# The last piece's residual on TensorE, shared pair products, and row tiles for the compressed values, in a two-mixer decoder layer

## The chip, the cores and the metric

One core of a Trainium2 chip runs the whole layer in one launch. The metric is the device time in microseconds (us), the median over runs. TensorE is written PE in the profile (its weight loads PEld), VectorE DVE, ScalarE ACT, GpSimd POOL; SP is the engine whose queue issues nearly all DMAs.

## The reference, cut to what matters

A sequence of 512 tokens, width 1024, passes one layer. One input projection `h = x @ w_in + b_in` feeds two token mixers and their gates; a sum goes through one output projection, a residual and a layer norm:

```python
o_a = nsa_attention(...) * silu(z_a)            # mixer A, 8 heads of 64
o_b = rmsnorm(hgrn2(q_b, f_b, i_b)) * silu(z_b) # mixer B, 4 heads of 128
y = sigmoid(gm_a) * (o_a @ w_branch_a) + sigmoid(gm_b) * (o_b @ w_branch_b)
out = layer_norm(alpha * x + y @ w_out, ln_g, ln_b)
```

Mixer A sums three attentions (compressed blocks, selected blocks, window) with gates per head. The compressed branch has 31 keys and values per group of four heads, made by a small network from blocks of 32 tokens: `pc = masked_softmax(q @ kc.T * scale)`, then `pc @ vc`. Mixer B works in chunks of 64 tokens with the running sum b of the log forget gates in a chunk: `attn = tril(qe @ ke.T)` with `qe = q * exp(b)`, `ke = k * exp(-b)`, `o = attn @ v`, and a state carried from chunk to chunk.

## The kernel before, in words

Sequence positions lie on the free axis as 4 tiles of 128. The large products are made of three TensorE matmuls in the rounded type fp32r, from values split into hi (`A.copy`, a cast on ACT) and lo (`V.tensor_tensor`, the rest, on DVE) by `split2`: hi*hi, hi*lo, lo*hi. Smaller products are plain fp32; the trace shows each of those as two matmul records.

TensorE's instructions and all DMAs keep the order of the program; on ACT and DVE a scheduler places them. The program's backbone is a row of weight tiles: `proj` (line 254) takes tile i, loads tile i+3 into one of three stream buffers, splits tile i+2 and issues 24 matmuls. Inside it `weave.tick()` runs after every 6 matmuls: generators (`hgrn`, `cmp_kv`, `cmp_scores`, `attn_scores`, `attn_values`) put their own instructions there, and the table `D` (line 67) says after how many ticks each goes on. The time of a matmul group in this stream is thus laid out by hand.

`hgrn` (line 364) treats one head of mixer B. Chunks come in pairs of 64 columns. For the products inside pairs, lines 403 to 408 issue six fp32 matmuls: two of 128 columns for the first chunks (weights `ke`), four of 64 columns for the second (weights `e1`). Masked copies on DVE (lines 410 to 415) put the causal part into `attn_sb`.

`cmp_kv` (line 498) makes the compressed keys `kcB` and values. The values are copied by eight small instructions into the block tile `vcB` (128 x 512, zero elsewhere, lines 529 to 536) and split into hi and lo (540). `cmp_probs` makes probabilities and splits them. `attn_values` (line 683) then makes four outputs of 128 x 512, each by three fp32r matmuls of 512 columns (lines 688 to 695), one output per tick.

After the 16 gate tiles (lines 836 to 842) comes the loop over `BRANCH` (line 873): eight tiles of branch weights, each 24 matmuls, order b b b a a b a a. Each output is evacuated on DVE (line 892); those of branch a are added to b (896) and split into y[kt] (898). In the same loop the output weights are loaded (`load_out(n)`, 877), and two tiles later `split_out(n - 2)` (864) takes each row's mean away (ACT with accumulation, 859; 861), casts hi (ACT, 868) and makes lo (DVE, 869). `split_out(6)` and `split_out(7)` come behind the loop. Taking row means from weights and residual makes the rows of the sum have mean zero, so the layer norm has only a scale to find.

The last stage (line 918) has four token tiles tt. Tile 0 runs kt by kt for both halves at once; the others half by half. The last tile is cut into 512, 256 and 256 columns. Behind each piece DVE adds the residual (937), takes statistics (938) and multiplies by the gain (940). At the end: aggregate (942), square root on ACT (945), reciprocal (946), the gain for the last piece (948), two normalizing instructions of 512 columns (950) and a store of 256 KB after each. Working tiles come from a pool `t2` of 67 buffers, PSUM from four pools of two banks: pa, pss, pst, pso.

Of the kernel before, what the change touches and what calls it, by code (L numbers as in the profile page):

```python
# [9 lines left out]
F32 = mybir.dt.float32  # L10
# [12 lines left out]
EPS = 1e-5  # L23

# [22 lines left out]
def _columns(name):  # L47

    c = np.arange(_COLS[name], _COLS[name] + 128)
    if name[0] == "q" and name[1] != "b" or name[:2] == "za":  # L50
# [17 lines left out]
         r0=5, p0=4, p1=11, p2=2, b0=1, a0=1, a1=1, a2=1, a3=1, a4=2, a5=1, s0=17, s2=0, s3=1)  # L68
# [27 lines left out]
def layer_kernel(ctx: ExitStack, tc: tile.TileContext, xT, xn, w0, wi, wf, wv, small, brow, consts,  # L96
# [145 lines left out]
    vcB = cst.tile([P, 4, 128], F32, name="vcB")  # L242
    G.memset(vcB, 0.0)
# [120 lines left out]
    def hgrn(h):  # L364
# [3 lines left out]
        bc, kc, qc = chunks(b), chunks(k), chunks(qs[h])  # L368
# [9 lines left out]
        yield D["h2"]  # L378
        A.activation(e2, e2, AF.Exp)
        A.activation(e1, e1, AF.Exp)  # L380
        A.activation(eb, b, AF.Exp)
        ke = T2(256)
        kev = ke.rearrange("p (t s) -> p t s", s=64)
        A.activation(kev, bc[:, :, 0], AF.Exp, scale=-1.0)
# [5 lines left out]
        qeM, qeo = T2(), T2(256)  # L390
        ebc, qmc = chunks(eb), chunks(qeM)
        qov = qeo.rearrange("p (t s) -> p t s", s=64)
# [17 lines left out]
        for v in range(2):  # L410
            V.copy_predicated(chunks(at[0:64])[:, v:4:2, 0],
                              tri[0:64, 0:64].unsqueeze(1).to_broadcast([64, 2, 64]),
                              chunks(pst_[64 * v:64 * v + 64])[:, v:4:2, 0])
        V.copy_predicated(chunks(at)[:, :, 1], tri[:, 64:128].unsqueeze(1).to_broadcast([P, 4, 64]),
                          chunks(pst_)[:, :, 1])
# [23 lines left out]
        A.activation(sq, po, AF.Square)  # L439
        A.copy(o, po)  # L440
# [55 lines left out]
    mvs, ready, vcp = [None, None], set(), []  # L496

    def cmp_kv():
# [30 lines left out]
        for g in range(2):  # L529
            for m in range(4):  # L530
                r = 32 * (2 * (m % 2) + g)
                dst, src = vcB[r:r + 32, m, 64 * g:64 * g + 64], ps[r:r + 32, 64 + 64 * g:128 + 64 * g]
                if m % 2:
                    V.tensor_copy(dst, src)
                else:
                    A.copy(dst, src)
# [56 lines left out]
    def cmp_scores():  # L593

        while "cmp" not in ready:
            yield 1
        pg = PS(), PS()
        for m in range(4):
            for g in range(2):
                gs = slice(64 * g, 64 * g + 64)  # L600
                T.matmul(pg[g][32 * m:32 * m + 32], kcB[gs], qraw[m][gs], start=True, stop=True)
        sT = T2(), T2()
        A.copy(sT[0], pg[0])
        V.tensor_copy(sT[1], pg[1])
        yield D["p2"]
        ss = T2(), T2()
        s6 = [s.rearrange("p (i m g n) -> p g i m n", i=4, m=2, g=2) for s in ss]
        for g in range(2):
            ps = transpose4(sT[g])
            p4 = ps.rearrange("p (i c m n) -> p c i m n", i=4, c=2, m=2)  # L610
            for c in range(2):
                V.tensor_tensor(s6[c][:, g], p4[:, c], cmask.unsqueeze(2).to_broadcast([P, 4, 2, 32]), ALU.add)
            yield 1
        for c in range(2):
            weave.start(cmp_probs(c, ss[c]), 2 * c)

    def cmp_probs(c, s):
        s3 = s.rearrange("p (x n) -> p x n", n=32)
        mx = SM(16, "mx")
# [8 lines left out]
        for m in range(2):  # L628
            mxm = mx.rearrange("p (i m g) -> p i m g", i=4, m=2)[:, :, m]
            V.tensor_tensor(mxm, mxm, gv.rearrange("p i (g m) b -> p i g m b", g=2)[:, :, :, 2 * c + m, 0], ALU.mult)  # L630
# [3 lines left out]
        PTc[c] = T2(dt=F32R), T2(dt=F32R)  # L634
        split2(ps, *PTc[c])
# [47 lines left out]
    def attn_values():  # L683
# [3 lines left out]
        yield D["b0"]  # L687
        for m in range(4):
            po = PO()
            hi, lo = (t[:, 128 * m:128 * m + 128] for t in vcp)  # L690
            T.matmul(po, hi, PTc[m // 2][0], start=True, stop=False)
            T.matmul(po, hi, PTc[m // 2][1], start=False, stop=False)
            T.matmul(po, lo, PTc[m // 2][0], start=False, stop=True)
            A.copy(asum[:, m], po)
            yield 1
# [139 lines left out]
    gm = {}  # L835
    for i in range(8):
        for c in "ab":
            name = "g%s%d" % (c, i)
            ps, m = proj(name)
            gm[name] = T2()  # L840
            with tc.issue_after(exps[-1]):
                A.activation(gm[name], ps, AF.Tanh, bias=hbias[:, m:m + 1], scale=0.5)


    wo, woraw = [], {}
    lg, lbn = [T2(), T2()], [T2(), T2()]

    def load_out(kt):
        if kt < 8:
# [13 lines left out]

    def split_out(kt):
        hl = [(T2(dt=F32R), T2(dt=F32R)) for _ in range(2)]
        nm = minus_mean(woraw[kt])
# [4 lines left out]

    y, rb = [], {}
    for n, (mix, m0) in enumerate(BRANCH):
# [3 lines left out]
        load_out(n)  # L877
# [22 lines left out]
        if n >= 2:  # L900
            split_out(n - 2)
    split_out(6)
    split_out(7)
# [14 lines left out]
    for tt in range(4):  # L918
        c = slice(128 * tt, 128 * tt + 128)
        last = tt == 3  # L920
        cuts = [(0, 0, 512), (1, 0, 256), (1, 256, 512)] if last else [(0, 0, 512), (1, 0, 512)]
        bst = SM(6 * len(cuts), "bst")
        xr = res[tt]
        bank = (PT, PO, PA, PS)[tt]
        pso_ = [bank() for _ in cuts[:2]] + ([PT()] if last else [])
        seq = [(u, kt) for u in range(len(cuts)) for kt in range(8)]
        if tt == 0:
            seq = [(u, kt) for kt in range(8) for u in range(2)]
        for u, kt in seq:
            hf, a, b = cuts[u]  # L930
            hi, lo = wo[kt][hf]
            ps = pso_[u][:, 0:b - a]
# [3 lines left out]
            if kt == 7:  # L936
                V.scalar_tensor_tensor(xr[hf][:, a:b], ps, 0.5, xr[hf][:, a:b], ALU.mult, ALU.add)
                V.bn_stats(bst[:, 6 * u:6 * u + 6], xr[hf][:, a:b])  # L938
                if not (last and u == 2):
                    V.tensor_tensor(xr[hf][:, a:b], xr[hf][:, a:b], lg[hf][:, a:b], ALU.mult)  # L940
        ag = SM(2, "ag")
        V.bn_aggr(ag, bst[:, 0:6 * len(cuts)])
# [4 lines left out]
        if last:  # L947
            V.tensor_tensor(xr[hf][:, a:b], xr[hf][:, a:b], lg[hf][:, a:b], ALU.mult)
# [84 lines left out]
```

## Time and profile before

| | us |
|---|---|
| median of 3 runs | 438.39 (437.7 to 438.88) |
| the profiled execution | 437.94 |
| its span in the profile | 436.1 |
| around the span | 1.84 |
| PE busy | 428.6 (98% of the span) |
| DVE / ACT / POOL busy | 304.3 / 245.2 / 16.3 |
[...]

The span is from the first to the last instruction on the core. Matmuls are pipelined, so their single durations overlap; the chain of waits gives the time of a group of them in the stream. The time of a line is read from the view that groups instructions by line and shape.

### The profile page before, as it was taken

To read this page: it belongs to the slowest core of one execution; us is meant where nothing else is said; L and a number is where in the kernel's file an instruction comes from. 1 tells how busy PE (TensorE), PEld (TensorE's weight loads), DVE (VectorE), ACT (ScalarE), POOL (GpSimd) and SP (SyncE) were. 2 spreads that over 40 slices of the span, in tenths; PEclk is the share of its full clock that TensorE was granted. 3 is DMA by queue.
4 is the path that set the end of the run, shared out by engine and by line. 5 is a ranking of instruction groups with operands and counts; after the bars stand their busy time and mean duration, and the time that the engine had idled before them with its cause. 6 is when DMAs were issued, how large, how long until landed. Compare 5 with 4: busy or idle time off the path is not lost.

```text
span 436.1 us, 6086 instructions
## 1 busy us (share of the span) xinstructions
PE 428.6 (98%) x2185; PEld 359.6 (82%) x2185; DVE 304.3 (70%) x629; ACT 245.2 (56%) x490; POOL 16.3 (4%) x27
## 2 busy tenths in 40 slices
PE   9999999999999999999999999999999999999994
PEld 8888888888898878888888888888888888877884
DVE  5915669986887577976665666578755768875395
ACT  4434624613447553768866666688864646569300
POOL 2000000000010220000000010001001100000000
PEclk9999999999999999999999999999999999999998
DMA  8995400352330554132112211111212462153022
GB/s 270 396 357 173 176 0 1 86 145 74 114 95 0 170 155 157 51 116 78 48 48 59 87 51 48 50 48 48 99 48 98 167 220 87 57 157 134 1 102 92
DMA packets 20879, 47.57 MB, mean 109 GB/s; under 512 B 2929, under 2 KB 4593, under 8 KB 20849
## 3 DMA queue, kind: packets, MB, share of 16 engines
q1 hardware_dynamic: 20560, 46.92, 32.1%
q8 instruction: 17, 0.28, 0.3%
q10 hardware_dynamic: 288, 0.26, 0.2%
q14 instruction: 14, 0.11, 0.1%
HBM read 41.93 MB, written 2.10 MB: 101 GB/s over the span
## 4 chain that ended last, share of the span: by engine, by line
PE 93%; DVE 5%; ACT 1%; issue 0%; DVEq 0%; ACTq 0%
PE pa L104 59%; PE pss L104 15%; PE pso L104 12%; PE pst L108 5%; PE pst L104 2%; DVE t L869 1%; DVE t L892 1%; DVE t L148 1%; ACT t L147 1%; DVE t L896 1%; DVE wlo L148 0%; DVE t L950 0%; DVEq L1029 0%; DVE sm_nm L861 0%; DVE sm_bst L938 0%
## 5 line engine op out<-in xcount | busy, mean ns | idle before, releaser
L104 PE MATMUL pa<-t,whi 128*128 128x512 f32 x640 | 201.6, 396 | 0.0
L104 PEld LDWEIGHTS pa<-t,whi 128*128 128x128 f32 x640 | 117.0, 188 | 24.5 <-issue 1.2
L104 PE MATMUL pa<-t,wlo 128*128 128x512 f32 x320 | 125.1, 391 | 0.0
L104 PEld LDWEIGHTS pa<-t,wlo 128*128 128x128 f32 x320 | 60.1, 188 | 13.1
L147 ACT CAST whi<-wraw 128x1024 fp32r<-128x1024 f32 x46 | 48.2, 1047 | 33.7 <-PE pa L104 20.1
L148 DVE TENSOR_TENSOR wlo<-wraw,whi 128x1024 fp32r<-128x1024 f32 x46 | 57.8, 1261 | 12.0 <-ACT whi L147 11.8
L664 DVE CUSTOM_DVE_ANT_0 t<-pss,t 128x512 f32<-128x512 f32 (+3 forms) x64 | 30.1, 488 | 24.0 <-PE pss L104 24.0
L148 DVE TENSOR_TENSOR t<-pst,t 128x512 fp32r<-128x512 f32 x42 | 28.9, 690 | 17.3 <-ACT t L147 17.2
L667 ACT ACTIVATE t<-t,sm_mn 128x512 f32<-128x512 f32 (+3 forms) x64 | 35.8, 560 | 9.1 <-DVE sm_mn L664 7.4
L104 PE MATMUL pso<-t,t 128*128 128x512 f32 (+2 forms) x170 | 36.9, 352 | 0.0
L104 PE MATMUL pa<-t,t 128*128 128x512 f32 (+1 forms) x168 | 36.7, 375 | 0.0
L104 PE MATMUL pss<-t,t 128*128 128x512 f32 (+4 forms) x238 | 36.1, 307 | 0.0
L147 ACT CAST t<-pst 128x512 fp32r<-128x512 f32 x42 | 24.3, 579 | 20.4 <-PE pst L108 20.3
L104 PEld LDWEIGHTS pa<-t,t 128*128 128x128 f32 x168 | 30.3, 188 | 5.6
L104 PEld LDWEIGHTS pss<-t,t 128*128 128x128 f32 (+1 forms) x238 | 29.3, 176 | 3.7 <-DMA wraw<-in_wf_dram 0.4
L104 PEld LDWEIGHTS pso<-t,t 128*128 128x128 f32 x170 | 28.2, 196 | 4.2
L108 PE MATMUL pst<-con,t 128*128 128x128 f32 x189 | 28.6, 272 | 0.0
L108 PEld LDWEIGHTS pst<-con,t 128*128 128x128 f32 x189 | 23.2, 141 | 4.2 <-DVE t L148 0.2
L148 DVE TENSOR_TENSOR t<-t,t 128x512 fp32r<-128x512 f32 (+1 forms) x22 | 14.2, 666 | 13.5 <-ACT t L147 13.4
L104 PE MATMUL pso<-t,vv 128*128 128x512 f32 x80 | 23.1, 410 | 0.0
L147 ACT CAST t<-t 128x512 fp32r<-128x512 f32 (+1 forms) x22 | 12.7, 603 | 12.9 <-DVE t L896 12.7
L104 PE MATMUL pss<-t,whi 128*128 128x512 f32 x64 | 19.7, 389 | 0.0
(164 smaller groups left out, 532.5 us busy)
## 6 DMA issues: line engine op xcount, KB each, us to landing
wraw<-in_wf_dram SPq DMA_DIRECT2D x38, 512.0 KB, 3.6
wraw<-in_wbr_dram SPq DMA_DIRECT2D x8, 512.0 KB, 3.5
t<-in_wout_dram SPq DMA_DIRECT2D x16, 256.0 KB, 3.8
t<-in_w_dram SPq DMA_DIRECT2D x15, 256.0 KB, 5.5
t<-t SPq DMA_DIRECT2D x48, 64.0 KB, 2.0
t<-in_wi_dram SPq DMA_DIRECT2D x8, 256.0 KB, 6.1
t<-in_xn_dram SPq DMA_DIRECT2D x8, 256.0 KB, 7.1
out_dram<-t SPq DMA_DIRECT2D x8, 256.0 KB, 2.1
```

The costliest lines, as they stand in the source:

```text
L104: return tc.keep_in_program_order(nc.tensor.matmul(*a, **k))
L108: return tc.keep_in_program_order(nc.tensor.transpose(*a, **k))
L147: A.copy(dst_hi, src)
L148: V.tensor_tensor(dst_lo, src, dst_hi.bitcast(F32), ALU.subtract)
L664: V.tensor_tensor_reduce(out=p[:, c], in0=ps[:, c], in1=amask[:, 512 - n:512], op0=ALU.add, op1=ALU.min, scale=-0.125, scalar=3.0e38, accu ...
L667: A.activation(p[:, c], p[:, c], AF.Exp, bias=mn[:, k], scale=-1.0, accum_out=den[:, k])
L869: V.scalar_tensor_tensor(lo, raw, nm, hi.bitcast(F32), ALU.add, ALU.subtract)
L892: V.scalar_tensor_tensor(r, gm["g%s%d" % (mix, m)], 1.0, ps, ALU.add, ALU.mult)
L896: V.tensor_tensor(r, r, rb[m], ALU.add)
```

## The change

1. Mixer B: the first chunk's query is scaled by exp(-(b_end - b)) and by 2^-64 (`FIRST`), so that both chunks of a pair use the same weights `e1`: four fp32 matmuls of 128 columns and one masked copy of 128 x 512. The output of first chunks is scaled back when it leaves PSUM.
2. Compressed values: one copy to a 128 x 128 `vcB`; probabilities stay fp32, in rows 32m + n per group; eight fp32 matmuls with 32 rows, 64 weight columns and 512 moving columns, into four banks (two of pso, two of pst), and four copies behind them.
3. Output weights: load, row mean and split of each kt are issued three tiles earlier; the first begin in the gate loop, the last split stands at BRANCH tile 6.
4. The last piece: twice the residual is split into hi and lo and added by TensorE with an identity (two more matmuls of 256 columns); ACT sums the squares from PSUM; DVE applies the gain from PSUM. Squares of the other two pieces are also summed on ACT instead of DVE statistics. Four normalizing instructions of 256 columns and four stores of 128 KB.
5. `D["s0"]`, the delay of `attn_scores`, is 18 ticks for 17.

```diff
+AHEAD = 1
+FIRST = 2.0 ** -64
...
-        ke = T2(256)
-        A.activation(kev, bc[:, :, 0], AF.Exp, scale=-1.0)
+        A.activation(qpc[:, :, 0], chunks(e1)[:, :, 0], AF.Exp, scale=-1.0)
...
-        V.tensor_tensor(qov, qc[:, :, 1], ebc[:, :, 1], ALU.mult)
-        V.tensor_tensor(kev, kev, kc[:, :, 0], ALU.mult)
-        V.tensor_tensor(qmc[:, :, 0], qc[:, :, 0], ebc[:, :, 0], ALU.mult)
-        V.tensor_tensor(qmc[:, :, 1], qov, ebc[:, :, 0, 63:64].to_broadcast([P, 4, 64]), ALU.mult)
+        V.tensor_tensor(qpc[:, :, 1], qc[:, :, 1], ebc[:, :, 1], ALU.mult)
+        V.scalar_tensor_tensor(qpc[:, :, 0], qc[:, :, 0], FIRST, qpc[:, :, 0], ALU.mult, ALU.mult)
+        V.scalar_tensor_tensor(qmc[:, :, 0], qc[:, :, 0], FIRST, ebc[:, :, 0], ALU.mult, ALU.mult)
+        V.tensor_tensor(qmc[:, :, 1], qpc[:, :, 1], ebc[:, :, 0, 63:64].to_broadcast([P, 4, 64]), ALU.mult)
...
-        for u in range(2):
-            T.matmul(chunks(pst_)[:, 2 * u:2 * u + 2, 0], ke[:, 128 * u:128 * u + 128],
-                     qmc[:, 2 * u:2 * u + 2, 0], start=True, stop=True)
         for t in range(4):
-            T.matmul(pst_[:, 128 * t + 64:128 * t + 128], e1[:, 128 * t:128 * t + 128],
-                     qeo[:, 64 * t:64 * t + 64], start=True, stop=True)
+            c = slice(128 * t, 128 * t + 128)
+            T.matmul(pst_[:, c], e1[:, c], qp[:, c], start=True, stop=True)
...
-        A.activation(sq, po, AF.Square)
-        A.copy(o, po)
+        A.activation(chunks(o)[:, :, 0], chunks(po)[:, :, 0], AF.Identity, scale=1.0 / FIRST)
+        A.copy(chunks(o)[:, :, 1], chunks(po)[:, :, 1])
+        A.activation(sq, o, AF.Square)
...
-        for g in range(2):
-            for m in range(4):
-                r = 32 * (2 * (m % 2) + g)
...
+        A.copy(vcB, ps[:, 64:192])
         ready.add("cmp")
-        yield 2
-        vcp.extend((T2(dt=F32R), T2(dt=F32R)))
-        split2(vcB.rearrange("p m d -> p (m d)"), *vcp)
...
-        PTc[c] = T2(dt=F32R), T2(dt=F32R)
-        split2(ps, *PTc[c])
+        PTc[g] = T2()
+        A.copy(PTc[g], ps)
...
+        pc = [PO(), PO(), PT(), PT()]
+        for g in range(2):
+            for m in range(4):
+                rows = slice(32 * m, 32 * m + 32)
+                T.matmul(pc[m][64 * g:64 * g + 64], vcB[rows, 64 * g:64 * g + 64], PTc[g][rows],
+                         start=True, stop=True)
         for m in range(4):
-            po = PO()
-            hi, lo = (t[:, 128 * m:128 * m + 128] for t in vcp)
-            T.matmul(po, hi, PTc[m // 2][0], start=True, stop=False)
-            T.matmul(po, hi, PTc[m // 2][1], start=False, stop=False)
-            T.matmul(po, lo, PTc[m // 2][0], start=False, stop=True)
-            A.copy(asum[:, m], po)
-            yield 1
+            A.copy(asum[:, m], pc[m])
+        yield 1
...
+    def out_ahead(n):
+        n += AHEAD
+        load_out(n + 2)
+        if 0 <= n < 8:
+            split_out(n)
+        if 0 <= n + 1 < 8:
+            mean_out(n + 1)
...
+            out_ahead(2 * i + "ab".index(c) - 16)
...
-        load_out(n)
...
-        if n >= 2:
-            split_out(n - 2)
-    split_out(6)
-    split_out(7)
+        out_ahead(n)
...
+    V.tensor_copy(eye, ident)
+    A.activation(r2h, rlast, AF.Identity, scale=2.0)
+    V.scalar_tensor_tensor(r2l, rlast, 2.0, r2h.bitcast(F32), ALU.mult, ALU.subtract)
...
+        V.scalar_tensor_tensor(xr[hf][:, a:b], ps, 0.5, xr[hf][:, a:b], ALU.mult, ALU.add)
+        A.activation(junk[:, 0:b - a], xr[hf][:, a:b], AF.Square, accum_out=ss[:, u:u + 1])
+        V.tensor_tensor(xr[hf][:, a:b], xr[hf][:, a:b], lg[hf][:, a:b], ALU.mult)
+    V.tensor_scalar(ss[:, 0:1], ss[:, 0:1], 1.0 / DM, EPS, ALU.mult, ALU.add)
+    V.scalar_tensor_tensor(ss[:, 1:2], ss[:, 1:2], 1.0 / DM, ss[:, 0:1], ALU.mult, ALU.add)
+    ps = PT()[:, 0:256]
+    run = outputs(ps, 3, 1, 256, 512)
+    next(run)
+    T.matmul(ps, eye, r2h, start=False, stop=False)
+    T.matmul(ps, eye, r2l, start=False, stop=False)
+    for _ in run:
+        pass
+    with tc.issue_after(nat):
+        A.activation(junk[:, 0:256], ps, AF.Square, scale=0.5, accum_out=ss[:, 2:3])
+        A.activation(ss[:, 3:4], ss[:, 2:3], AF.Sqrt, scale=1.0 / DM, bias=ss[:, 1:2])
+    V.scalar_tensor_tensor(rlast, ps, 0.5, lg[1][:, 256:512], ALU.mult, ALU.mult)
+    V.reciprocal(ss[:, 3:4], ss[:, 3:4])
+    for hf, a, b in ((0, 0, 256), (0, 256, 512), (1, 0, 256), (1, 256, 512)):
+        V.scalar_tensor_tensor(xr[hf][:, a:b], xr[hf][:, a:b], ss[:, 3:4], lbn[hf][:, a:b], ALU.mult, ALU.add)
+        dma(out[384:512, 512 * hf + a:512 * hf + b], xr[hf][:, a:b])
```

`outputs` issues the same three matmuls per kt as before for one piece; `mean_out` is the first half of the old `split_out`.

## Rows read from the trace of the kernel before

**Rows 1.** The page: busy time of each engine, share of the span, instructions.

```profile
PE 428.6 (98%) x2185; PEld 359.6 (82%) x2185; DVE 304.3 (70%) x629; ACT 245.2 (56%) x490; POOL 16.3 (4%) x27
```

**Rows 2.** The page: the chain that ended last, by engine.

```profile
PE 93%; DVE 5%; ACT 1%; issue 0%; DVEq 0%; ACTq 0%
```

**Rows 3.** Chain of waits, 68 to 140 us: start, length, what, records.

```profile
76.52 1.29 PE pss L104 x12
...
90.47 0.67 PE pss L104 x6
...
136.82 0.99 PE pss L104 x8
```

**Rows 4.** Chain of waits, whole span, around the compressed branch.

```profile
161.18 1.38 PE pss L104 x16
...
199.15 0.68 PE pso L104 x3
```

**Rows 5.** Stretches: busy (instructions) of PE, PEld, DVE, ACT, POOL; then clock, DMA share, GB/s.

```profile
330.00:340.00 10.00, 10.00 (x49) 8.17 (x48) 4.47 (x7) 4.06 (x7) 0.00 (x0) 1.00 0.41 142
350.00:360.00 10.00, 10.00 (x46) 8.28 (x45) 5.74 (x10) 4.31 (x9) 0.00 (x0) 1.00 0.66 213
390.00:400.00 10.00, 9.72 (x42) 7.51 (x41) 6.59 (x12) 9.20 (x18) 0.00 (x0) 1.00 0.60 216
434.00:435.00 1.00, 0.00 (x0) 0.00 (x0) 0.00 (x0) 0.00 (x0) 0.00 (x0) 0.50 0.76 285
```

**Rows 6.** Timeline, 391 to 396 us: start, length, what, [idle before, releaser].

```profile
392.05 4.07 DVE L869 SCALAR_TENSOR_TENSOR t<-t,sm_nm,t 128x512 fp32r<-128x512 f32 x6
392.06 0.19 PEld L104 LDWEIGHTS pst<-t,t 128*128 128x128 f32 x1 [0.33 <-ACT t L868]
392.85 3.32 PEld L104 LDWEIGHTS pst<-t,t 128*128 128x128 f32 x15 [0.60 <-DVE t L869]
```

**Rows 7.** Chain of waits, 380 to 437 us: its end.

```profile
427.12 2.89 PE pst L104 x24
...
430.04 0.44 DVE t L937
...
431.23 0.30 ACT sm_rs L945
...
431.56 0.17 DVE sm_rs L946
```

**Rows 8.** Groups by line and shape: busy, mean ns | idle before.

```profile
L439 ACT ACTIVATE t<-pso 128x512 f32<-128x512 f32 x4 | 2.4, 599 | 7.6 <-PE pso L104 7.6
L937 DVE SCALAR_TENSOR_TENSOR t<-pss,t 128x512 f32<-128x512 f32 x1 | 0.7, 685 | 0.0
L937 DVE SCALAR_TENSOR_TENSOR t<-pst,t 128x256 f32<-128x256 f32 x1 | 0.4, 425 | 1.5 <-PE pst L104 1.5
```

**Rows 9.** Timelines: ACT with accumulation; DVE's last work; SP's last stores; SP's loads.

```profile
299.02 0.50 ACT L667 ACTIVATE t<-t,sm_mn 128x256 f32<-128x256 f32 x1
299.42 0.19 ACT L667 ACTIVATION_READ_ACCUMULATOR t<-t,sm_mn 128x1 f32 x1
...
431.76 1.42 DVE L950 SCALAR_TENSOR_TENSOR t<-t,sm_rs,t 128x512 f32<-128x512 f32 x2
...
432.54 0.99 SPq L111 DMA_DIRECT2D out_dram<-t  x2
...
385.61 0.38 SPq L111 DMA_DIRECT2D t<-in_lng_dram  x1
386.08 0.38 SPq L111 DMA_DIRECT2D t<-in_lnb_dram  x1
```

**Rows 10.** The stores: issue (min/median/max ns) and landing (us); ACT's table loads.

```profile
L111 SPq DMA_DIRECT2D out_dram<-t x8: 332/333/348, 415.5 to 433.2; - x8
...
DMA to landing us min/median/max: 2.0/2.1/3.6
...
L144 ACT ACT_TABLE_LOAD x6 | 7.7, 1283 | 1.7 <-PEq L1021 1.7
```

More of the change, by code (lines that the diff above doesn't have):

```diff
@@ L241, in layer_kernel @@
     asum = cst.tile([P, 4, 512], F32, name="asum")
-    vcB = cst.tile([P, 4, 128], F32, name="vcB")
-    G.memset(vcB, 0.0)
+    vcB = cst.tile([P, 128], F32, name="vcB")
     split(0)
@@ L494, in cmp_hidden @@
         mvs[a] = mv
-    mvs, ready, vcp = [None, None], set(), []
+    mvs, ready = [None, None], set()
     def cmp_kv():
@@ L832, in layer_kernel @@
         zs[name] = z
[L835 to L842, printed above, removed]
     wo, woraw = [], {}
-    lg, lbn = [T2(), T2()], [T2(), T2()]
     def load_out(kt):
-        if kt < 8:
+        if 0 <= kt < 8:
             woraw[kt] = [T2(), T2()]
@@ L870, in split_out @@
         wo.append(hl)
+    def out_ahead(n):
[5 more added lines that the diff above has]
+            mean_out(n + 1)
+    gm = {}
+    for i in range(8):
+        for c in "ab":
+            name = "g%s%d" % (c, i)
+            ps, m = proj(name)
+            gm[name] = T2()
+            with tc.issue_after(exps[-1]):
+                A.activation(gm[name], ps, AF.Tanh, bias=hbias[:, m:m + 1], scale=0.5)
+            out_ahead(2 * i + "ab".index(c) - 16)
     y, rb = [], {}
+    lg, lbn = [T2(), T2()], [T2(), T2()]
     for n, (mix, m0) in enumerate(BRANCH):
@@ L917, in layer_kernel, with outputs @@
             A.activation(res[tt][hf], res[tt][hf], AF.Identity, bias=nm)
-    for tt in range(4):
-        c = slice(128 * tt, 128 * tt + 128)
[L920 to L930, printed above, removed]
+    eye, r2h, r2l = T2(128, F32R), T2(256, F32R), T2(256, F32R)
+    rlast = res[3][1][:, 256:512]
+    V.tensor_copy(eye, ident)
+    A.activation(r2h, rlast, AF.Identity, scale=2.0)
+    V.scalar_tensor_tensor(r2l, rlast, 2.0, r2h.bitcast(F32), ALU.mult, ALU.subtract)
+    def outputs(ps, tt, hf, a, b):
+        c = slice(128 * tt, 128 * tt + 128)
+        for kt in range(8):
             hi, lo = wo[kt][hf]
-            ps = pso_[u][:, 0:b - a]
             T.matmul(ps, y[kt][0][:, c], hi[:, a:b], start=kt == 0, stop=False)
@@ L935, in layer_kernel @@
             T.matmul(ps, y[kt][1][:, c], hi[:, a:b], start=False, stop=kt == 7)
[L936 to L940, printed above, removed]
+            yield kt
+    for tt in range(3):
+        bst = SM(12, "bst")
+        xr = res[tt]
+        bank = (PT, PO, PA)[tt]
+        pso_ = bank(), bank()
+        runs = [outputs(pso_[hf], tt, hf, 0, 512) for hf in range(2)]
+        if tt == 0:
+            for _ in zip(*runs):
+                pass
+        for hf in range(2):
+            for _ in runs[hf]:
+                pass
+            V.scalar_tensor_tensor(xr[hf], pso_[hf], 0.5, xr[hf], ALU.mult, ALU.add)
+            V.bn_stats(bst[:, 6 * hf:6 * hf + 6], xr[hf])
+            V.tensor_tensor(xr[hf], xr[hf], lg[hf], ALU.mult)
         ag = SM(2, "ag")
-        V.bn_aggr(ag, bst[:, 0:6 * len(cuts)])
+        V.bn_aggr(ag, bst[:, 0:12])
         rs = SM(1, "rs")
@@ L946, in layer_kernel @@
         V.reciprocal(rs, rs)
-        if last:
-            V.tensor_tensor(xr[hf][:, a:b], xr[hf][:, a:b], lg[hf][:, a:b], ALU.mult)
         for hf in range(2):
             V.scalar_tensor_tensor(xr[hf], xr[hf], rs[:, 0:1], lbn[hf], ALU.mult, ALU.add)
-            dma(out[c, 512 * hf:512 * hf + 512], xr[hf])
+            dma(out[128 * tt:128 * tt + 128, 512 * hf:512 * hf + 512], xr[hf])
+    xr, ss, junk = res[3], SM(4, "ss"), T2()
+    for u, (hf, a, b) in enumerate(((0, 0, 512), (1, 0, 256))):
+        ps = PS()[:, 0:b - a]
+        for _ in outputs(ps, 3, hf, a, b):
+            pass
+        V.scalar_tensor_tensor(xr[hf][:, a:b], ps, 0.5, xr[hf][:, a:b], ALU.mult, ALU.add)
[9 more added lines that the diff above has]
+    for _ in run:
+        pass
+    with tc.issue_after(nat):
[6 more added lines that the diff above has]
+        dma(out[384:512, 512 * hf + a:512 * hf + b], xr[hf][:, a:b])
 def _constants():
```

50 lines of the change are left out of this document (20 added, 30 removed).

## The prediction

> **What bounds the kernel now.** I read the page first: PE is busy for 98% of the span and DVE, the next, for 70% [rows 1]. A busy PE is only modelled, so the chain of waits comes next: it runs over PE for 93% [rows 2]. [...] So PE's stream is the bound: a matmul taken out of it shortens the run by its place in the chain, and work of DVE, ACT, POOL and SP counts only where PE waits for it or after PE's last matmul. There are two such places. At 391 to 393 us PE's weight loads stand idle for 0.33 and 0.60 us behind the output weights' splits [rows 6]; the stretch from 390 us has 41 weight loads where 45 are usual [rows 5]. And behind the last matmul about 6 us run through DVE, ACT, DVE, a store and the closing barrier [rows 7, 9].
>
> **1. Pair products, in PE's stream.** The six fp32 matmuls of one head are 12 records and take 1.29 us; three fp32 matmuls of 128 columns elsewhere are 6 records and take 0.67 [rows 3]. A record thus costs 0.11 us whether it has 64 columns or 128: half the columns don't halve it. Four matmuls of 128 columns are 8 records, 0.89 us. Saved: 4 heads x 0.40 = 1.6 us. Ends: 1.2 (a little lost where groups join) and 1.8 (16 records at 0.11). ACT and DVE work here changes by a few tenths per head (one large masked copy for three; ACT evacuates the output in two halves before it squares); it stands beside TensorE's products as it does now. Were that cover gone, PE would wait under 0.5 us a head.
>
> **2. Compressed values, in PE's stream.** Now four times 0.68 us of fp32r [rows 4], 2.72. After: eight fp32 matmuls with 32 rows and 64 weight columns. The trace has none of that form, but two neighbours: four fp32 matmuls of 32 columns, side by side in the array, take 0.99 us [rows 3]; eight with 64 rows and 32 columns take 1.38 [rows 4], which may hold a wait. One 512-column fp32 matmul by itself would be 4 x 0.22 = 0.89 by the group of three in [rows 3], so both neighbours ran side by side. I take 1.2, between them: saved 1.5. Ends here: 1.3 and 1.7; a group that runs one by one is a rival below. The four copies follow in a row, 0.6 us each like the ACT pass over PSUM in [rows 8], and hold both pst banks for some 2.4 us; the first attention transposes, which want them next, come more than a whole weight tile later in the stream. If that cover is gone, PE waits up to 2.4 us once. The eight small copies, one split, POOL's clearing and the probabilities' lo parts leave DVE and ACT: nothing gained, PE didn't wait for them.
>
> **3. Output weights three tiles earlier.** Per kt this is about 2.5 us of ACT and 1.5 of DVE. The two waits above, 0.93 less the usual 0.04 twice, are what it removes; I take 0.8, with ends 0 and 0.9 (four missing loads at 0.22). The six last lo parts, 4.07 us of DVE [rows 6], move in front of that point; DVE is busy only 5.74 of 10 us from 350 and 4.47 from 330 us [rows 5], so they fit. Late next would be y[6] and y[7]; the first output tile takes kt in order, and y[7] isn't needed for 7 x 6 matmuls, some 9.5 us. What else is issued earlier: 16 loads on SP, each right behind a branch-weight load. SP keeps program order, so a load that waits for a free buffer holds the branch weights behind it. By the code some 60 of 67 buffers are alive near the end of attention (my count), and 2 to 6 more are wanted: they fit, narrowly. I cost it at nothing; the cover is that loads run two to three tiles, 11 to 16 us, ahead of PE. Without it PE would wait for a branch weight.
>
> **4. The last piece, behind PE.** PE's own part grows by two matmuls of 256 columns: 2 x 2.89/24 = 0.24 us [rows 7]. The identity, r2h and r2l are made long before and hide beside earlier tiles. Then the chain. Now, from DVE's first instruction at 430.04 to the first normalizing one at 431.76: 1.72 us [rows 7, 9]. After: square with accumulation on ACT; the same pair over 256 columns takes 299.02 to 299.61 = 0.59 [rows 9], somewhat less from PSUM without a bias operand, so 0.5; square root 0.30, reciprocal 0.17 and three hand-overs of 0.02 to 0.03 [rows 7]: 1.05. Saved 0.67. DVE's gain from PSUM, 0.43 [rows 8], runs beside it. Then normalizing: 256 columns cost 0.26 less than 512 (685 less 425 ns [rows 8]), so 0.49 for 0.75, and with the overlap that two of 512 show (1.42 for 1.50 [rows 9]) the four end after 0.49 + 3 x 0.41 = 1.72. The stores don't keep that pace: SP issues loads that come in a row 0.475 us apart [rows 9]. First issue 0.52 after normalizing begins, last 0.52 + 3 x 0.475 = 1.95. Now the last issue is at 432.54 + 0.99 - 0.33 = 433.20 [rows 9, 10], that is 1.44. Lost: 0.5. If SP did 0.33 each, DVE would set it at 1.75, lost 0.3. The landing now takes 2.0 to 2.1 us for 256 KB [rows 10]. While these bytes move, 285 GB/s at a share of 0.76 means 375 at full share [rows 5]: 256 KB take 0.70, half of it 0.35. So 128 KB land up to 0.35 earlier, or no earlier if four stores get in each other's way: I take 0.3. Sum of the end: +0.24 - 0.67 + 0.5 - 0.3 = -0.25; ends -0.8 and +0.4.
>
> [...]
>
> **5. Attention one tick later.** A quarter tile, twice the 0.68 of [rows 4] or six matmuls. Attention's products stand before the branch loop, and the first tile that needs them is that loop's fourth, so three tiles cover the shift: nothing. If they didn't, PE would wait 1.4 us.
>
> **Sum:** 1.6 + 1.5 + 0.8 + 0.25 = 4.15 us. The profiled execution took 437.94 (span 436.1 and 1.84 around it): 433.8. The median of the runs is 0.45 above that execution, so for the median 438.39 - 4.15 = **434.2 us**. All ends good: 1.8 + 1.7 + 0.9 + 0.8 = 5.2, or 433.2. All bad: 1.2 + 1.3 + 0 - 0.4 = 2.1, or 436.3. About 0.3% (1.3 us) is what a measurement of this kernel can tell from no change.
>
> **Rivals.**
> *The ends don't pay.* The wait at 391 us only changes its releaser (y[6], y[7] or DVE's longer queue in place of the weights) and four stores cost 0.3: 1.6 + 1.5 - 0.3 = 2.8, 435.6 us. For it: ACT was busy 9.20 of 10 us from 390 [rows 5], with y's own splits among the rest, and ACT and DVE hand to each other there. Against it: the idle shares from 330 and 350 us in the same rows. Chance 0.11.
>
> *Square needs another table on ACT.* A table load takes 1.283 us [rows 10]. If Square is outside the set loaded for the square root, one load comes before it and one behind it on the final chain: +2.6, a gain of 1.6, 436.8 us. Against it: Square at line 439 shows idle time only for PE [rows 8], and the six table loads are those the program asks for; but that is under another set. [...] Chance 0.04.
>
> *Row tiles don't overlap* (the change doesn't do what it says there). If only the two 64-column halves run side by side, the group takes 4 x 0.89 = 3.6 us: part 2 loses 0.9 and the gain is 1.75, 436.6; with the wait kept as well, under 1, or 437.4. Chance of that last, no measurable change, 0.06.
>
> *Slower.* The same place, one mechanism: all eight run one after the other, 8 x 0.89 = 7.1 us for 2.72. Part 2 costs 4.4; 1.6 - 4.4 + 0.8 + 0.25 is +1.75: 440.1 us. It decides from a group of about 6.7 us on. For it: no instruction of this form is in the trace, and fp32 goes in two passes. Against it: the groups with 64 rows, and with 32 columns, ran side by side [rows 3, 4]. With a branch weight held on SP (part 3) this is what could make it slower. Chance 0.04.
>
> **How the numbers follow.** The forecast has 0.75, its rivals 0.11, 0.04, 0.06 and 0.04. Faster: 0.75 + 0.11 + 0.04 = 0.90; same 0.06; slower 0.04. The range takes in the forecast's ends with the runs' spread of half a us below, and the first rival above: 432.7 to 436.3.
>
> **What would show it.** Right: 8 records and about 0.9 us for a head's pair products; 16 records for the compressed values in 1.0 to 1.4 us; 45 weight loads in every 10 us up to the output stage, with no wait for line 869's successor; about 1.05 us from the last matmul to the first normalizing instruction, then four stores some 0.47 us apart, the last landing in about 1.75. Wrong: a compressed group above 2.7 us, PE waiting for branch weights in the gate or branch tiles, a table load behind 427 us, or stores that land later than 2.1 us.

## The result and the profile after

The changed kernel takes 434.69 us (median of 6 runs, 433.47 to 435.12) where the kernel before, on the same chip, takes 438.65 (6 runs, 437.7 to 439.35): a ratio of 0.9914, 95% interval 0.9898 to 0.9929, so 4.0 us faster (3.1 to 4.5). Run once more later (after_again below) it gave 433.97 (5 runs) where the kernel before, beside it, took 437.51: 0.9915 (0.9896 to 0.9935). The forecast was 434.2, a change of 4.2.

The profiled execution of the changed kernel took 435.12 us with a span of 433.3, the longest of its six. Against the span of 436.1 before only 2.8 us are gone in this pair of profiles; where the rest is will be seen below.

The page, its busy times and the chain by engine, which answer to [rows 1, 2]:

```profile
PE 426.2 (98%) x2175; PEld 356.5 (82%) x2175; DVE 297.9 (69%) x611; ACT 246.7 (57%) x497; POOL 16.3 (4%) x26
...
PE 98%; DVE 0%; issue 0%; DVEq 0%; ACT 0%; ACTq 0%
```

DVE and ACT have left the chain except at its very end. TensorE is the bound more purely than before. The chain of waits (start, length, what, records), to be held against [rows 3, 4, 7]:

```profile
7.28 1.43 PE pss L107 x12
...
77.06 0.89 PE pss L107 x8
77.95 5.49 PE pa L107 x24
...
159.92 2.02 PE pss L107 x16
...
193.09 1.36 PE pa L107 x6
194.45 0.57 PE pso L107 x2
...
195.50 1.58 PE pa L107 x6
...
424.41 3.13 PE pst L107 x26
427.54 0.02 issue
...
428.66 0.48 DVE t L979
```

The same view of the kernel before, at places that the rows ahead of the prediction don't show:

```profile
6.72 1.44 PE pss L104 x12
...
77.81 5.52 PE pa L104 x24
```

What is to be seen, in order of time. Lengths are differences of these rows and of [rows 3, 4, 7].

- **Start:** the second group of matmuls begins at 7.28 in place of 6.72. Of the change only POOL's clearing of `vcB` falls there; TensorE waits for a cast on ACT that waits for a load of the input, 0.96 us at 3.90 (before: 0.45 us at 3.39), so the first loads landed later in this execution. +0.56.
- **Pair products:** 0.89 us and 8 records for 1.29 and 12, four times (at 77.06, 83.77, 91.14 and 102.75): -1.60. The weight tiles behind them also got shorter, 5.49 for 5.52 and in the other three 0.05, 0.06 and 0.07: -0.2. Together -1.8.
- **The compressed keys' score products:** 2.02 us for 1.38 [rows 4]. The change doesn't touch them: +0.64.
- **Compressed values:** one group from 194.45 to 195.50, 1.05 us, and a slower restart behind it (1.58 us for six records that usually take 1.36), where four times 0.68 stood [rows 4]: 2.72 - 1.05 - 0.22 is -1.45.
- **Output stage:** no wait is left in front of it, -0.8, and two matmuls more, 3.13 us for 2.89: +0.24.
- **End:** from the last matmul's end to the end of the span 5.8 us (433.3 - 427.54) where it was 6.1 (436.1 - 430.01): -0.3.

The sum is -2.9, and the spans differ by 2.8. Without the later start the change is worth 3.3 to 3.4 in this execution; had the score products kept their 1.38 us, it would be 4.0.

The compressed values in TensorE's timeline (start, length, what):

```profile
194.38 0.64 PE L107 MATMUL pso<-t,vcB 32*64 32x512 f32 x2
...
194.91 0.59 PE L107 MATMUL pst<-t,vcB 32*64 32x512 f32 x2
195.43 0.73 PE L107 MATMUL pa<-t,whi 128*128 128x512 f32 x2
```

There are eight such rows of two records (here the first and the last); four start within 0.05 us from 194.38 on, four within 0.04 from 194.87 on. By the order of the program the first four hold one record of each of the eight matmuls and the other four the second records: the eight tiles of the array work side by side.

The stretches that answer to [rows 5], same columns:

```profile
350.00:360.00 10.00, 10.00 (x46) 8.29 (x45) 9.48 (x16) 6.57 (x14) 0.00 (x0) 1.00 0.50 159
390.00:400.00 10.00, 10.00 (x46) 8.29 (x45) 2.57 (x7) 8.67 (x20) 0.00 (x0) 1.00 0.23 88
```

From 390 us the weight loads are 45 in place of 41 [rows 5]. The splits went to the stretch from 350, where DVE is now busy for 9.48 us of 10, and TensorE's 45 loads there are not disturbed.

The last four stores: SP's issues on the timeline, then their issue times (ns, min/median/max) and landing (us), as in [rows 10]; and ACT's table loads, the last of them by the timeline:

```profile
429.17 1.79 SPq L114 DMA_DIRECT2D out_dram<-t  x4
...
L114 SPq DMA_DIRECT2D out_dram<-t x4: 333/384/398, 429.2 to 430.6; - x4
...
DMA to landing us min/median/max: 1.7/1.8/1.8
...
L147 ACT ACT_TABLE_LOAD x6 | 7.7, 1283 | 1.7 <-PEq L1050 1.7
...
390.55 1.28 ACT L147 ACT_TABLE_LOAD   x1
```

Six table loads as before, the last at 390.55: Square needs none at the end.

### The profile page after: what moved, and what is told of

Same layout as the page of the kernel before. It is cut to its first block, busy times and chain, and to the rows that moved or that the text cites. A ratio compares the mean times of both kernels' runs of the same rounds, so it can differ in the third digit from the quotient of the medians.

```text
span 433.3 us, 6068 instructions
## 1 busy us (share of the span) xinstructions
PE 426.2 (98%) x2175; PEld 356.5 (82%) x2175; DVE 297.9 (69%) x611; ACT 246.7 (57%) x497; POOL 16.3 (4%) x26
## 4 chain that ended last, share of the span: by engine, by line
PE 98%; DVE 0%; issue 0%; DVEq 0%; ACT 0%; ACTq 0%
PE pa L107 61%; PE pss L107 17%; PE pso L107 12%; PE pst L111 5%; PE pst L107 3%; DVE t L979 0%; DVE t L976 0%; DVEq L1058 0%; ACT t L974 0%; DVE t L162 0%; DVE sm_ss L977 0%; ACTq L974 0%
## 5 line engine op out<-in xcount | busy, mean ns | idle before, releaser
L151 DVE TENSOR_TENSOR wlo<-wraw,whi 128x1024 fp32r<-128x1024 f32 x46 | 56.9, 1241 | 22.4 <-ACT whi L150 22.2
L151 DVE TENSOR_TENSOR t<-pst,t 128x512 fp32r<-128x512 f32 x40 | 27.5, 690 | 15.8 <-ACT t L150 15.8
L107 PE MATMUL pss<-t,t 128*128 128x512 f32 (+3 forms) x222 | 34.5, 310 | 0.0
L150 ACT CAST t<-pst 128x512 fp32r<-128x512 f32 x40 | 23.2, 580 | 18.9 <-PE pst L111 18.8
L107 PE MATMUL pso<-t,t 128*128 128x512 f32 (+2 forms) x158 | 33.6, 350 | 0.1
L107 PEld LDWEIGHTS pss<-t,t 128*128 128x128 f32 (+1 forms) x222 | 27.5, 174 | 3.7 <-issue 0.7
L107 PEld LDWEIGHTS pso<-t,t 128*128 128x128 f32 x158 | 26.2, 199 | 4.0 <-ACT t L183 0.4
```

The lines of the kernel that those rows point to most:

```text
L107: return tc.keep_in_program_order(nc.tensor.matmul(*a, **k))
L150: A.copy(dst_hi, src)
L151: V.tensor_tensor(dst_lo, src, dst_hi.bitcast(F32), ALU.subtract)
```

## The experiments

The variants ran in three groups, each on one chip with the kernel before beside it. Differences from the changed kernel are taken between ratios, at 437.5 us and against 0.9915. By the intervals each ratio is uncertain by 0.6 to 0.9 us, the changed kernel's too, and a difference of two thus by about 1 us. So only pairs_before, ahead_before and s3_two differ from the changed kernel by more than that, and the profiles carry the smaller terms.

| kernel | median us | ratio to before | interval | from the changed kernel |
|---|---|---|---|---|
| pairs_before | 435.99 | 0.9951 | 0.9934 to 0.9967 | +1.6 |
| cmp_before | 434.94 | 0.9929 | 0.9909 to 0.9948 | +0.6 |
| ahead_before | 436.66 | 0.9970 | 0.9955 to 0.9984 | +2.4 |
| late_weights | 434.85 | 0.9934 | 0.9917 to 0.9951 | +0.8 |
| tail_before | 434.85 | 0.9926 | 0.9907 to 0.9945 | +0.5 |
| two_stores | 433.41 | 0.9905 | 0.9891 to 0.9918 | -0.4 |
| three_stores | 433.99 | 0.9916 | 0.9902 to 0.9929 | 0.0 |
| act_stores | 434.62 | 0.9930 | 0.9916 to 0.9943 | +0.7 |
| s3_2 | 433.41 | 0.9903 | 0.9890 to 0.9917 | -0.5 |
| norm_dve | 434.36 | 0.9918 | 0.9898 to 0.9939 | +0.1 |
| s3_two | 432.66 | 0.9886 | 0.9867 to 0.9906 | -1.3 |
| after_again | 433.97 | 0.9915 | 0.9896 to 0.9935 | 0 |

**Pair products undone (pairs_before).**

Here cut to the matmuls; the scaling, the masked copies and the evacuation on ACT are undone with them.

```diff
+        for u in range(2):
+            T.matmul(chunks(pst_)[:, 2 * u:2 * u + 2, 0], ke[:, 128 * u:128 * u + 128],
+                     qmc[:, 2 * u:2 * u + 2, 0], start=True, stop=True)
         for t in range(4):
-            c = slice(128 * t, 128 * t + 128)
-            T.matmul(pst_[:, c], e1[:, c], qp[:, c], start=True, stop=True)
+            T.matmul(pst_[:, 128 * t + 64:128 * t + 128], e1[:, 128 * t:128 * t + 128],
+                     qeo[:, 64 * t:64 * t + 64], start=True, stop=True)
```

> The changed kernel with the pair products done as before (six fp32 matmuls, twelve records a head, in place of four with eight). Theory, the path sum: each head costs TensorE 1.29 us in place of 0.89, four heads stand in TensorE's stream, so the time is 1.6 us above the changed kernel (1.2 to 1.8), about 436.2 us. Rival: the compressed keys' products wait longer in the changed kernel because the pair products now leave TensorE earlier than ACT and DVE can follow; then part of the 1.6 is given back there, and undoing the part costs only about 1.0 us.

Measured: +1.6 us. The chain of waits of this kernel has the older rows again:

```profile
76.41 1.29 PE pss L107 x12
77.70 5.52 PE pa L107 x24
...
161.06 1.96 PE pss L107 x16
```

The score products are as long as in the changed kernel, so they can be that long without the new pair products, and the rival falls. What lengthens them comes below.

**Compressed values undone (cmp_before).**

Cut to the products; the eight small copies, the splits and the older probabilities come back with them.

```diff
...
-                T.matmul(pc[m][64 * g:64 * g + 64], vcB[rows, 64 * g:64 * g + 64], PTc[g][rows],
-                         start=True, stop=True)
...
+            T.matmul(po, hi, PTc[m // 2][0], start=True, stop=False)
+            T.matmul(po, hi, PTc[m // 2][1], start=False, stop=False)
+            T.matmul(po, lo, PTc[m // 2][0], start=False, stop=True)
```

> The changed kernel with mixer B's compressed values as before (full-width probabilities, twelve fp32r matmuls, values padded with zeros and split), the attention one tick later as in the changed kernel. Theory: four groups of 0.68 us stand where one of 1.0 to 1.1 us stood, so the time is 1.4 to 1.7 us above the changed kernel, about 436.2 us. Rival: the eight small copies, the split and the probabilities' lo parts of the older form delay DVE and ACT and the wait of the compressed keys' products changes with them, to more than 2 us or to less than 1 us above.

Measured: +0.6 us in the runs, less than the 1.4 to 1.7 that the theory asks for; the runs don't show the part's price. Its chain of waits shows why one number is not enough:

```profile
158.72 1.02 PE pss L107 x16
...
195.87 0.68 PE pso L107 x3
```

The four groups of 0.68 are back (the first of them is shown), with the 1.4 to 1.5 us that they cost; but in this execution the score products held 1.02 us, 1.0 less than in the changed kernel's profile. The two make 0.45, and the runs say 0.6. The rival named such a change of the wait. The price of the part is thus read from the rows alone; whether this form of the kernel has the short score products in all executions or had them here by chance, one profile can't say.

**Output weights three tiles later (ahead_before), then exactly as before (late_weights).**

```diff
-AHEAD = 1
+AHEAD = -2
...
         out_ahead(n)
+    out_ahead(8)
+    out_ahead(9)
```

> The changed kernel with the output weights' loads, means and splits three tiles later, as before. Theory: the wait of TensorE's weight loads in front of the output stage comes back, 0.8 us above the changed kernel (0.5 to 0.9), about 435.5 us. Rival: the wait was that of the mixers' sums and would be there with either order, so the time is the same within 0.2 us.

Measured: +2.4 us, three times the theory. TensorE's weight loads and ACT in the timeline of ahead_before (in brackets the idle time before, and its releaser):

```profile
390.65 1.93 PEld L107 LDWEIGHTS pst<-t,t 128*128 128x128 f32 x9 [0.60 <-DVE t L848]
393.10 0.30 PEld L107 LDWEIGHTS pst<-t,t 128*128 128x128 f32 x2 [0.52 <-DVE t L848]
394.04 0.19 PEld L107 LDWEIGHTS pst<-t,t 128*128 128x128 f32 x1 [0.64 <-ACT t L847]
394.83 1.00 PEld L107 LDWEIGHTS pst<-t,t 128*128 128x128 f32 x5 [0.60 <-DVE t L848]
...
393.27 1.34 ACT L847 ACTIVATE t<-t,sm_nm 128x512 fp32r<-128x512 f32 x2 [0.39 <-DVE sm_nm L835]
```

Five waits in place of the two of [rows 6], 2.63 us with one of 0.27 ahead of these. ACT waits 0.39 us for the last mean, which it computes here between the last splits; in the kernel before and in late_weights it does so ahead of the last six casts. The loads of the output weights also stand at the end of a tile's products here and at their start there. So it is no clean undoing. late_weights has the older functions and order whole:

```diff
-        nm = wmean[kt]
+        nm = minus_mean(woraw[kt])
...
-            out_ahead(2 * i + "ab".index(c) - 16)
...
+        load_out(n)
...
-        out_ahead(n)
+        if n >= 2:
+            split_out(n - 2)
+    split_out(6)
+    split_out(7)
```

> The changed kernel with the output weights handled exactly as before: load, mean and split in the branch loop, the last two tiles' splits behind it, each mean inside its split. Theory: weight loads stand idle for about 0.9 us in front of the first output tile as before, 0.8 us above the changed kernel; the 2.2 us of the earlier undo came from its order, which put the last mean between the last splits. Rival: it costs 2 us here too, because the changed kernel's shorter stream leaves DVE and ACT less time ahead of that point.

Measured: +0.8 us, and the two waits of [rows 6] are back to the hundredth:

```profile
388.59 0.19 PEld L107 LDWEIGHTS pst<-t,t 128*128 128x128 f32 x1 [0.32 <-ACT t L847]
389.38 3.74 PEld L107 LDWEIGHTS pst<-t,t 128*128 128x128 f32 x17 [0.60 <-DVE t L848]
```

The theory holds by these rows: 0.92 us of waiting, less the usual 0.04 twice, and the runs' 0.8 fits. ahead_before waits 1.7 us more (2.63 for 0.92); the rows put that down to the late mean, and whether the later loads have a part in it wasn't tried.

**The last piece undone (tail_before).**

```diff
-    T.matmul(ps, eye, r2h, start=False, stop=False)
-    T.matmul(ps, eye, r2l, start=False, stop=False)
...
-    for hf, a, b in ((0, 0, 256), (0, 256, 512), (1, 0, 256), (1, 256, 512)):
...
+            dma(out[c, 512 * hf:512 * hf + 512], xr[hf])
```

> The changed kernel with the last row tile as before (residual and moments on DVE, one aggregation, two normalizing instructions and two stores of 256 KB). Theory: the end loses 0.25 to 0.35 us, of which the sum holds 0.24 for two matmuls less and about 0.6 for the longer chain behind them; about 435.0 us. Rival: the four stores cost what the shorter chain gives, and the older end is 0.1 to 0.3 us faster.

Measured: +0.5 us, too uncertain to part the theory from the rival. The profile decides:

```profile
424.17 2.89 PE pst L107 x24
```

Its last matmul ends at 424.17 + 2.89 = 427.06 and its span at 433.2, so 6.1 us lie behind it, against 5.8; with 0.24 us of matmuls less, the older end is slower by 0.1 alone. The part was worth less than forecast.

**Two, three stores, and stores from two engines (two_stores, three_stores, act_stores).**

```diff
-    for hf, a, b in ((0, 0, 256), (0, 256, 512), (1, 0, 256), (1, 256, 512)):
...
+    for hf in range(2):
+        V.scalar_tensor_tensor(xr[hf], xr[hf], ss[:, 3:4], lbn[hf], ALU.mult, ALU.add)
+        dma(out[384:512, 512 * hf:512 * hf + 512], xr[hf])
```

That is two_stores. three_stores has the pieces `((0, 0, 512), (1, 0, 256), (1, 256, 512))`; in act_stores ACT issues every second store.

> The changed kernel with two normalizing instructions of 512 columns and two stores of 256 KB at the end in place of four and four. Theory: last issue 1.44 us after normalizing begins and landing 2.05 later, 3.49, against 1.90 and 1.78 = 3.68 in the changed kernel: 0.2 us faster. Rival: four smaller stores start the first bytes earlier and the landing of 256 KB is the longer term; 0.2 us slower.

> The changed kernel with normalizing and stores of 512, 256 and 256 columns at the end. Theory: one store less on SP; first issue about 0.7 us after normalizing begins, last about 1.7, landing 1.75 later, 3.45 against 3.68: 0.2 us faster, and no slower than two stores. Rival: SP is not what spaces the stores, DVE is, and nothing changes within 0.1 us.

> The changed kernel with its four last stores issued in turn by SP and ACT. Theory: SP's issue of 0.47 us a store spaces them; with two issuers DVE's 0.41 does, the last issue comes 1.75 in place of 1.90 us after normalizing begins, 0.15 us faster. Rival: the second queue's store lands later than SP's, and the time is the same or up to 0.3 us longer.

Measured in the runs: -0.4, 0.0 and +0.7, with intervals that overlap; they don't order the three. Behind the last matmul the profiles give 5.5 us for two stores (span 431.4, last matmul's end 425.88), 5.5 for three (432.5, 426.97) and 5.5 for act_stores (432.5, 426.96), against 5.8 for the four, in the changed kernel's two profiles and in the six variants that keep them. So each is some 0.3 better than the four at that place, as expected for two and three, a little more than expected for act_stores; its longer time has its cause ahead of the end, at least in its profile: it has the long score products (2.0 us), two_stores hasn't (1.0). The end of two_stores, its chain, its issues and its landing:

```profile
425.88 0.02 issue
...
427.00 0.75 DVE t L979
...
427.78 0.99 SPq L114 DMA_DIRECT2D out_dram<-t  x2
...
DMA to landing us min/median/max: 2.0/2.0/2.1
```

Its last issue is 1.44 us after normalizing begins (427.78 + 0.99 - 0.33 - 427.00), as in the kernel before, against 1.9 for the four; the landing is 2.0 to 2.1 against 1.7 to 1.8. The later issue weighs more than the earlier landing.

**The longer score products (s3_2, after_again, norm_dve).** In the changed kernel's profile the score products' last quarter waits for ACT. POOL, DVE, ACT and TensorE's weight loads there, on the timeline:

```profile
156.52 1.77 POOL L466 TENSOR_TENSOR t<-t,t 128x512 f32<-128x512 f32 x1 [4.05 <-DMA t<-t]
...
157.06 1.78 DVE L570 TENSOR_TENSOR t<-t,t 128x512 f32<-128x512 f32 x1
...
158.87 1.26 ACT L573 CAST t<-t 64x512 fp32r<-64x512 f32 x2 [3.72 <-DVE t L570]
160.16 0.69 ACT L333 ACTIVATE t<-pa,sml 128x512 f32<-128x512 f32 x1
...
160.89 0.14 PEld L107 LDWEIGHTS pss<-t,kcB 64*32 64x32 f32 x4 [0.88 <-ACT t L333]
```

Read from below: the weights wait 0.88 us for ACT's evacuation of the last queries (L333), which stands behind two casts (L573), which waited for DVE's product (L570), which took 1.78 us; its neighbour of the same kind and size, L569, takes 0.68. Beside it runs POOL's product. The rows fit an exclusion: DVE's instruction starts 0.54 us after POOL's and ends 0.55 us after POOL's end (156.52 + 1.77 = 158.29; 157.06 + 1.78 = 158.84).

```diff
-         r0=5, ... s0=18, s2=0, s3=1)
+         r0=5, ... s0=18, s2=0, s3=2)
```

> The changed kernel with the attention's compressed scores one tick (a quarter of a weight tile) later in TensorE's order. In the changed kernel's profile the group of the compressed keys' score products holds 2.02 us where it held 1.38 before: TensorE waits for ACT's copy of the transposed queries, which stands behind two casts that wait for a slow DVE instruction. Theory: with one tick between, the wait goes, 0.6 to 1.0 us below the changed kernel, about 433.9 us. Rival: the wait is chance of one execution, or moves to the next transposes; same within 0.2 us.

Measured: -0.5 us, between the two. Its score products held 1.02 us, but in its profile DVE's product took 0.68, so that the wait would not have been there with either order: that profile tells nothing of the tick. Hence the changed kernel again, and one with POOL's product on DVE:

> The changed kernel once more, as the mark for the other runs on the same chip. In ten profiles so far DVE's product at line 570 (in the kernel before and in the variants its counterpart) took 0.68 us when POOL's product of line 466 started after it, and it or its neighbour 1.77 us when POOL's had started before it; the score products of the compressed keys then hold 2.0 us in place of 1.0. Theory: DVE waits until POOL's instruction has ended, and which comes first is decided by when POOL's data land, so an execution of this kernel either has the 1.0 us or not: 434.3 to 435.1 with it, about 433.5 without. Rival: the slow DVE instruction has another cause, and this profile shows it slow with POOL's product later than it, or fast with POOL's running before it.

Measured: 434.61 us in the profiled execution, with the wait; POOL's product started 0.12 us before DVE's, which took 1.78:

```profile
156.41 1.35 POOL L466 TENSOR_TENSOR t<-t,t 128x512 f32<-128x512 f32 x1 [4.52 <-DMA t<-t]
...
156.53 1.78 DVE L570 TENSOR_TENSOR t<-t,t 128x512 f32<-128x512 f32 x1
```

The five runs go from 432.98 to 434.70. late_weights, which is the same code up to the gates, gave the other case on the same chip:

```profile
156.55 1.84 POOL L466 TENSOR_TENSOR t<-t,t 128x512 f32<-128x512 f32 x1 [4.77 <-DMA t<-t]
...
156.56 0.68 DVE L570 TENSOR_TENSOR t<-t,t 128x512 f32<-128x512 f32 x1
...
159.35 0.18 PEld L107 LDWEIGHTS pss<-t,kcB 64*32 64x32 f32 x16 [0.35 <-issue]
```

Here both start within 0.01 us, DVE goes first, POOL takes 1.84 in place of 1.3, and TensorE loads all sixteen weights without a wait. Of all fourteen profiles seven have the long form (1.96 to 2.03 us), and in each of them POOL's product started 0.1 to 0.6 us before a product of DVE that then took 1.77 or 1.78. The theory holds, the rival falls.

```diff
-            G.tensor_tensor(o, o, rms[h], ALU.mult)
             yield 2
+            V.tensor_tensor(o, o, rms[h], ALU.mult)
```

> The changed kernel with the four products of line 466 on DVE, directly ahead of the instruction that follows them there, in place of POOL. Theory (DVE waits for POOL's instruction): no DVE instruction of the key computation takes 1.77 us in any execution, DVE is later by the moved 0.6 us alone, so TensorE's wait in the score products is 0 to 0.4 us in place of 0.9: 0.5 to 0.9 us faster than executions of the changed kernel that have the wait, about 434.0 us. Rival: the slow instruction is DVE's own, and stays at 1.77 us; no faster, or 0.5 us slower for the work moved to DVE.

```profile
156.90 0.68 DVE L570 TENSOR_TENSOR t<-t,t 128x512 f32<-128x512 f32 x1
...
159.65 0.14 PEld L107 LDWEIGHTS pss<-t,kcB 64*32 64x32 f32 x4 [0.36 <-ACT t L333]
```

The mechanism came out as expected: L570 takes 0.68, and TensorE waits 0.36 in place of 0.87 or 0.88, for the 0.6 us of work that DVE has more. The time shows no gain: +0.1 in the runs, uncertain by 1. It fits a changed kernel whose executions have the wait or not, while every execution of norm_dve pays the 0.36; but both profiles of the changed kernel have the wait, so that stays a guess. As a remedy it is a miss.

**Both remedies (s3_two):** one tick later and two stores.

> Compressed scores one tick later and two stores of 256 KB at the end, together. Theory: the tick covers DVE's wait for POOL in every execution (worth 1.0 us where it happens) and the two stores are worth 0.2: 0.8 to 1.2 us faster than the changed kernel in the median, about 433.4 us, and no execution above 434.3. Rival: both earlier medians were lower by chance, and it is the same as the changed kernel within 0.3 us.

Measured: 432.66 us, 0.9886 (0.9867 to 0.9906), four runs from 432.44 to 433.33; 1.3 us under the changed kernel's 433.97 beside it, whose interval (0.9896 to 0.9935) overlaps with its own. No execution is above 434.3, as expected. In its profile POOL was first:

```profile
155.21 1.80 POOL L466 TENSOR_TENSOR t<-t,t 128x512 f32<-128x512 f32 x1 [4.05 <-DMA t<-t]
...
155.78 1.78 DVE L570 TENSOR_TENSOR t<-t,t 128x512 f32<-128x512 f32 x1
...
159.93 0.18 PEld L107 LDWEIGHTS pss<-t,kcB 64*32 64x32 f32 x16 [0.35 <-issue]
```

This is what s3_2 couldn't show: DVE is held for the full 1.78 us, and the sixteen weights load without a wait, because the tick lies between. Its span of 430.6 is 2.2 under that of after_again (432.8): 1.0 from the score products, some 0.3 from the end, 0.76 from first loads that landed earlier (chance). It is faster than the kernel before; that it is faster than the changed kernel is likely by the rows, and not beyond doubt by the runs.

## Why the prediction was right, and where its terms were off

The time came out at 434.69 for 434.2, inside the range, and the change against the kernel before, run beside it, at 4.0 for 4.2. The forecast case held, and the rivals fell one by one: no table load at the end, the row tiles side by side, the wait at 391 us gone and not replaced (the four stores do cost 0.3 against two, but the end as a whole gains 0.1). The 0.3 us of the first rival is a net cost of the end, and no row or run shows it; what they showed in its place is that gain of 0.1. But one term was missing, and two were off by some 0.2 in opposite directions.

| term | forecast | measured | from |
|---|---|---|---|
| 1 pair products | -1.6 | -1.8; undone +1.6 | chain; pairs_before |
| 2 compressed values | -1.5 | -1.45; undone +0.6 in runs | chain; cmp_before has the four groups back, with a shorter wait elsewhere |
| 3 output weights | -0.8 | -0.8; undone +0.8 | stretch from 390; late_weights |
| 4 end | -0.25 | -0.1 | chain and span; tail_before |
| 5 attention a tick later | 0 | 0 to +0.1 | weight loads near 302 us idle 0.52 for 0.43 |
| score products | none | +0.64 or -0.36 | 2.02 or 1.02 for 1.38 |

- **Part 1, "a record costs 0.11 us whether it has 64 columns or 128":** right, 0.89 us a head to the hundredth. The 0.2 more came from the weight tiles right behind, which got shorter with it; pairs_before has the longer one back (5.52), but why it is longer wasn't tried. The upper end, 1.8, took it in for another reason.
- **Part 2, "I take 1.2, between them":** 1.05 and a restart of 0.22, so 1.27. Four copies on ACT hold the banks to 198.97 and nobody waits. Right.
- **Part 3:** the wait went, the loads on SP held no branch weight (45 weight loads in the stretches from 350 and 390 us), and y[6] and y[7] weren't late.
- **Part 4, the end:** the mechanism was right and three sizes were off by little. From the last matmul to normalizing 1.12 us (428.66 - 427.54) for a forecast 1.05, before 1.75: saved 0.63, forecast 0.67. Last issue 1.9 us after normalizing begins, forecast 1.95: lost 0.46, forecast 0.5. Landing 1.7 to 1.8, forecast 1.75, but before it was 2.0 for the last store rather than 2.05, so the gain is 0.2 and not 0.3. With +0.24 for the matmuls this leaves -0.1. What the prediction didn't ask is whether the older two stores could follow the shorter chain: two_stores does that, and is 0.3 better.
- **The missing term, "it stands beside TensorE's products as it does now":** the step that failed is that DVE's and ACT's work in front of the score products was put at nothing, where TensorE does wait for it. 1.38 us of the score products [rows 4] was read as what eight such matmuls take, "which may hold a wait". It did: undisturbed they take 1.02. Before, the wait was short; the rows of the kernel before, POOL and DVE 6 us ahead of the score products, are

```profile
154.60 1.29 POOL L469 TENSOR_TENSOR t<-t,t 128x512 f32<-128x512 f32 x1 [3.09 <-DMA t<-t]
...
155.28 1.70 DVE L148 TENSOR_TENSOR wlo<-wraw,whi 128x1024 fp32r<-128x1024 f32 x1 [2.08 <-ACT whi L147]
```

L148 usually takes 1.22 us; here POOL's product was running, and 0.48 came on top. From there DVE works without a gap into the product that ACT's casts wait for, and TensorE waits 0.23 us behind them; that the 0.48 is what makes this wait is read from the rows, no run tried it. POOL's next product started at 158.83, 0.06 us behind DVE's L583, and so too late to hold that. In the changed kernel's profile POOL's product came first. Whether the change makes that likelier, by shifting the loads that POOL waits for, stays open: the kernel before has one profile, and ten of the other thirteen run this stretch in the changed kernel's order with POOL's product, of which seven have the wait and three haven't. The terms that the forecast did have measure 1.8 + 1.45 + 0.8 + 0.1 = 4.15, its very sum; that it agrees so well is luck, since two errors cancel in it. With the score products the gain is some 3.3 us in executions with the wait (after_again's span is 432.8, the one before 436.1) and by the same 1.0 us some 4.3 in those without, of which the changed kernel itself has no profile; the 4.0 of the runs lies between. That the missing term didn't carry the time further off is luck as well.

## What to carry to other kernels

Where TensorE is the bound, count the records of small matmuls and not only their columns (64 columns cost what 128 do here, 0.11 us a record), and read a group's length in several executions before taking it for its cost: a wait of a microsecond was inside (2.02 us for 1.02). A product on POOL wasn't free beside DVE, whose 0.68 us became 1.78; if its start hangs on a transfer, put a tick of slack behind DVE's chain (no wait left in the profile of s3_two) rather than moving the work (0.36 us left in that of norm_dve). At a kernel's end, hold more and smaller stores against the pace of the issuing engine: here SP's four issues began 0.43 to 0.49 us apart where DVE's pieces began 0.40 apart, and 5.8 us lay behind the last matmul in place of 5.5 with two stores.

## What the runs showed of the hardware

- **DVE and POOL held each other up** in these products of two tiles in SBUF: DVE's 0.68 us (0.75 for line 468, which is 473 in pairs_before) becomes 1.77 or 1.78 when POOL's product began first, and POOL's 1.3 becomes up to 1.85 when a DVE instruction did (1.84 in late_weights, 1.85 in s3_2). The times fit an exclusion in both directions; what imposes it they don't show.
- **A store of 128 KB, issued by SP, landed in 1.7 to 1.8 us,** the first of four in a row in 1.7 and the others in 1.8, where one of 256 KB took 2.0 to 2.1; the two behind a store of 256 KB took 1.9 to 2.0 (three_stores).
- **Eight fp32 matmuls on 32 x 64 tiles of the array,** 512 columns each, take 1.05 us together, and the group behind them 0.22 us more than usual; three fp32 matmuls of 128 columns over the whole array take 0.67 [rows 3].
- **The start differs between executions:** TensorE's second group of products begins at 7.28 and 6.71 us in the changed kernel's two profiles, and at 5.95 in that of s3_two, whose code is the same up to there. Parts worth less than that are read from a profile, stretch by stretch, and not from a few runs.
